# The order of ACT and DVE in the expert steps of a two-layer backbone, set to the program's own from the first 64-slot step on

## The chip, the cores and the metric

The kernel runs on one core of a Trainium2 chip. The time is device time in microseconds (us), from a run of the whole program; the median of three runs is compared. Engines: PE is TensorE's matmul side and PEld its weight loads, DVE is VectorE, ACT is ScalarE, POOL is GpSimd, SP is SyncE, which here only issues DMAs.

## What is computed

Two layers over 256 latent and 256 context tokens of width 1024, in float32. Each layer mixes tokens (Fourier, neighbourhood attention, short convolution, gated and projected) and then channels. The channel mixer of layer 0 is a dense SwiGLU; that of layer 1, which the change touches, is a top-2-of-8 mixture on the 256 latent tokens:

```python
def moe(h, w_router, w_gate, w_up, w_down):
    logits = (h @ w_router).astype(jnp.float32)
    top_val, top_idx = lax.top_k(logits, TOP_K)
    top_w = jax.nn.softmax(top_val, axis=-1)
    gates = jnp.sum(jax.nn.one_hot(top_idx, N_EXPERTS, dtype=jnp.float32) * top_w[..., None],
                    axis=-2).astype(h.dtype)
    out = jnp.zeros_like(h)
    for e in range(N_EXPERTS):
        out = out + gates[..., e:e + 1] * swiglu(h, w_gate[e], w_up[e], w_down[e])
    return out
```

## The kernel before

The layers ahead of the experts fill the first half of the time (to about 1000 us) and are not touched. Then come the experts. Each expert's tokens are gathered into slots by a matmul with a one-hot matrix, go through SwiGLU, and are scattered back and added. Experts 0, 2, 4, 6 ("A") have 128 slots, experts 1, 3, 5, 7 ("B") have 64. The width 3584 is cut into seven slices (`FE`), so a step is one expert and one slice `(e, f)`, and there are 56 steps. `expert_steps` puts four A steps first (`LEAD = 4`), then B and A steps in turn, 24 pairs, then the four B steps that are left.

**Weights.** A step needs six tiles of 1 MB: two each of the gate, up and down weights (`g`, `u`, `d`). They stream through a ring of 15 buffers named `raw` (`RING` = 12, and three of the pool `wraw`), loaded by SP in the order of use: load n+15 is issued when the buffer of load n is free. All 336 loads are one queue.

**A steps.** A `raw` tile of an A step is used in two units of 1024 columns. `Net.split` (L184, L187) writes for each unit a rounded copy `wh` (a cast on ACT) and the rest `wl = raw - wh` (a subtraction on DVE). PE then does three matmuls for each product in `mm3` (L191 with `wh`, L192 with `wl`, L193 with `wh`), six for a unit. There are four pairs of `wh`, `wl` buffers. `Stream.make` writes the split of a unit into the program at the place where `Stream.next` frees a buffer, that is where the unit four places ahead has just been used up. `raw` is free when the second unit's subtraction is done.

**B steps.** They use `raw` as it is, with no split: L1242 for gate and up, L1282 for down.

**One step** (`run`): `gate_up` computes gate and up; ACT applies Silu to the gate (L171) and DVE multiplies by the up product (L1248). In the middle of the *next* step's gate half, `turn` transposes the product on PE (L1254) and copies it out (for A: cast on ACT, L184, and subtraction on DVE, L187, both into tiles named `t`; for B: a copy on ACT, L1261). After that next step's gate and up, `down` multiplies it by the down weights and adds up in PSUM. So PE's row of work over one pair is: gate and up of B, down of A, gate and up of the next A, down of B. The twelve split units of a pair (four of A's down, eight of the next A's gate and up) stand in one stretch on PE, called the A run below; the rest of a pair uses B's tiles. At an expert's end there are also `scatter`, `add`, and before the next pair of experts `choose` and `gather`.

**What sets the order.** The framework has a scheduler that orders each engine's instructions by its own plan. Inside `manual_schedule(engines=...)` (written `order(...)` here) the engines named keep the order in which the program writes their instructions; the others are still ordered by the scheduler. Before, the loop over the 56 steps stood under `order(PE)` alone; the tail after it stands under PE and ACT (`TAIL`). Each engine runs its own queue in order, and an instruction that waits holds up what stands behind it on its engine.

`run` is called twice. The second call lies in a branch that is taken only when an expert has more tokens than slots; in the profiled execution no instruction of it ran.

Of the kernel before, what the change touches and what calls it, by code (L numbers as in the profile page):

```python
# [1037 lines left out]
def experts(net, pre, mo, res, mods, route, rt, ident, ones, tri, iot, sel8):  # L1038
# [27 lines left out]
    def choose(e, kind, more):  # L1066


        if e % 2 == 0:
            ofs[e // 2] = mo.tile([P, 2, 2, P], F32R, tag="of", name="of", bufs=2)  # L1070
        of = ofs[e // 2][:, :, e % 2]
        base = (P if RANKS[e] is None else CAPS[RANKS[e]]) if more else 0
        for t in range(2):
            p = column(2 + t, e)
            if base:
                pb = mo.tile([P, 1], F32, tag="pb", name="pb", bufs=4)
                nc.vector.tensor_scalar(pb, p, -float(base), None, op0=ALU.add)
                p = pb
            o, i = of[:, t], iot
            if kind == "B":  # L1080
                o, i = o.rearrange("p (a b) -> p a b", a=2), iot[:, None, :P // 2].to_broadcast([P, 2, P // 2])
            mask = sel[:, t, 0:1] if RANKS[e] is None else column(t, e)
            nc.vector.tensor_scalar(o, i, p, mask, op0=ALU.is_equal, op1=ALU.mult)
# [92 lines left out]
    def gather(kinds, *places):  # L1176

        wide = [P if kinds[e] == "A" else P // 2 for e in places]
        m, c0 = sum(wide), places[0] % 2 * P
        of, n = ofs[places[0] // 2], 512 // m  # L1180
        for e in places:
            if kinds[e] == "B":
                xb[e] = mo.tile([P, KD, P // 2], F32, tag="xb", name="xb", bufs=2)
        for k0 in range(0, KD, n):
            pm, ks = net.bank(), range(k0, k0 + n)
            for k in ks:
                for j, r in enumerate(rows):
                    for t in range(2):
                        nc.tensor.matmul(pm[:, (k - k0) * m:(k - k0 + 1) * m], r[:, t, k * P:(k + 1) * P],  # L1189
                                         of[:, t].rearrange("p a b -> p (a b)")[:, c0:c0 + m],  # L1190
                                         start=j == t == 0, stop=j == t == 1)
            todo = [(e, k, pm[:, (k - k0) * m + i * wide[0]:][:, :w], mods[:, 3 * KD + k, 0:1])
                    for k in ks for i, (e, w) in enumerate(zip(places, wide))]
            for e, k, src, sh in todo:
                nc.scalar.activation(xa[0][:, k] if kinds[e] == "A" else xb[e][:, k], src, AF.Identity, bias=sh)
            for e, k, src, sh in todo:
                if kinds[e] == "A":
                    nc.vector.scalar_tensor_tensor(xa[1][:, k], src, sh, xa[0][:, k].bitcast(F32),
                                                   op0=ALU.add, op1=ALU.subtract)

    def prepare_end(e):

        of = ofs[e // 2][:, :, e % 2].bitcast(F32)
        pm = net.bank()
        for t in range(2):
            nc.tensor.transpose(pm[:, t * P:(t + 1) * P], of[:, t], ident)
        for t in range(2):
            nc.tensor.matmul(pm[:, 2 * P:2 * P + 1], of[:, t], column(4 + t, e), start=t == 0, stop=t == 1)
        oht = mo.tile([P, S], F32R, tag="oht", name="oht", bufs=2)
        nc.vector.tensor_copy(oht, pm[:, :S])  # L1210
        gs = mo.tile([P, 1], F32, tag="gs", name="gs", bufs=2)
        nc.vector.tensor_copy(gs, pm[:, 2 * P:2 * P + 1])
        return oht, gs

    def run(st, kinds, more, Sums):
# [7 lines left out]
        def gate_up(e, f, between):  # L1223
            pg = [net.bank(), net.bank()]
            t = sg[e, f] = net.t2()
            whole = kinds[e] == "B"
            n = 256 if whole else 512
            for i, name in enumerate("gu"):
                for kk in range(4):
                    if not whole:  # L1230
                        h, lo = st.next(name, e, f)
                        for j in range(2):
                            k, c = 2 * kk + j, slice(j * 512, j * 512 + 512)
                            net.mm3(pg[i], xa[0][:, k], xa[1][:, k], h[:, c], lo[:, c], k == 0, k == KD - 1)
                    else:

                        if kk % 2 == 0:
                            w = st.next(name, e, f)
                        for k in (2 * kk, 2 * kk + 1):
                            for j in range(2):  # L1240
                                c = (k % 4) * 512 + j * 256
                                nc.tensor.matmul(pg[i][j * half:(j + 1) * half, :256], xb[e][:, k], w[:, c:c + 256],  # L1242
                                                 start=k == 0, stop=k == KD - 1)
                    if (i, kk) in between:
                        between[i, kk]()
                if i == 0:
                    net.act(t[:, :n], pg[0][:, :n], AF.Silu)
            nc.vector.tensor_mul(t[:, :n], t[:, :n], pg[1][:, :n])  # L1248

        def turn(e, f):  # L1250
            pt = net.bank()
            n = 4 if kinds[e] == "A" else 2
            for j in range(n):
                nc.tensor.transpose(pt[:, j * P:(j + 1) * P], sg[e, f][:, j * P:(j + 1) * P], ident)  # L1254
            if n == 4:
                ih, il = net.t2(F32R), net.t2(F32R)
                net.split(ih, il, pt)
                parts[e, f] = ih, il
            else:
                x = parts[e, f] = net.t2()  # L1260
                nc.scalar.copy(x[:, :n * P], pt[:, :n * P])  # L1261
# [41 lines left out]
        def add(e, n):  # L1303

            oht, _ = ends[e]
            for q in (2 * n, 2 * n + 1):
                pm = net.bank()
                for j in range(2):
                    c = slice((2 * q + j) * P, (2 * q + j + 1) * P)
                    o = pm[:, j * S:(j + 1) * S]  # L1310
                    nc.tensor.matmul(o, y[e][:, 0, c], oht, start=True, stop=False)  # L1311
                    nc.tensor.matmul(o, y[e][:, 1, c], oht, start=False, stop=True)  # L1312
                for j in range(2):
                    k = 2 * q + j
                    nc.vector.scalar_tensor_tensor(
                        res[:, k], pm[:, j * S:(j + 1) * S], mods[:, 5 * KD + k, 0:1], res[:, k],
                        op0=ALU.mult, op1=ALU.add)

        order = lambda *engines: net.tc.manual_schedule(engines=set(engines))
        y = {}  # L1320
        with order(PE):
            for i, (e, f) in enumerate(steps):
                between, after = {}, []
                if i:
                    between[0, 1] = lambda: turn(*steps[i - 1])
                if i > 1 and steps[i - 2][1] == FE - 1:
                    for n in range(2):
                        between[0, 2 + n] = lambda n=n: add(steps[i - 2][0], n)
                if f == 2:
                    between[1, 1] = lambda: ends.update({e: prepare_end(e)})  # L1330
                if i == 0 and not more:
                    between[1, 1] = rest
                if "B" in kinds:

                    if i == 1:
                        between[1, 1] = lambda: choose(1, kinds[1], more)
                    if i == 2:
                        after.append(lambda: gather(kinds, 1))
                    if e % 2 == 0 and e < NE - 2 and f == 4:
                        between[1, 1] = lambda: [choose(x, kinds[x], more) for x in (e + 2, e + 3)]  # L1340
                    if e % 2 == 0 and e < NE - 2 and f == FE - 1:
                        after.append(lambda: gather(kinds, e + 2, e + 3))
                elif e < NE - 1:
                    if f == 4:
                        between[1, 1] = lambda: choose(e + 1, kinds[e + 1], more)
                    if f == FE - 1:
                        after.append(lambda: gather(kinds, e + 1))
                gate_up(e, f, between)
                for x in after:
                    x()  # L1350
                last = {}
                if i == len(steps) - 1:
                    last[0, 1] = lambda: turn(e, f)
                if i:
                    down(*steps[i - 1], last)
        with order(*TAIL):
            sums = Sums()
            down(*steps[-1])
# [107 lines left out]
```

## Time and profile before

| | us |
|---|---|
| median of three runs | 1886.62 (1885.18 to 1889.72) |
| the profiled execution, its own time | 1888.95 |
| its span, first to last instruction | 1887.2 |
| PE busy | 1836.3 (97%) |
| PEld busy | 1438.6 (76%) |
| DVE busy | 1174.3 (62%) |
| ACT busy | 816.8 (43%) |
| DMA, whole span | 514.69 MB, mean 273 GB/s |

The chain of work that ended last lies on PE for 95% of the span, on DVE for 3% and on ACT for 1%. In the page's slices the DMA engines are busy at 9 tenths and 390 to 420 GB/s from slice 24 on, which is the stage of the experts; the granted TensorE clock is at 9 tenths or more in every slice but the last.

A row of a busy group gives busy time, the mean of one instruction in ns, and the idle time of the engine just before it with what ended it. Matmuls overlap: a 128x512 matmul takes 0.39 us by its row, and the next one starts 0.23 us after it.

### The profile page before, as it was taken

How to read it: one execution, taken by the hardware profiler on the slowest of the kernel's cores; microseconds unless marked ns; L12 is line 12 of the kernel's file. 1: busy time of each engine (PE TensorE's matmuls, PEld its weight loads, DVE VectorE, ACT ScalarE, POOL GpSimd, SP SyncE). 2: the span in 40 equal slices, each digit the busy share in tenths (PEclk: the TensorE clock that was granted, in tenths of full speed). 3: DMA queues.
4: the chain of work that ended last, by engine and by line, in shares of the span. 5: the costliest groups of instructions: out<-in, count | busy, mean ns of one | idle time of the engine just before them, and what ended most of it. 6: DMA issues, size and time to landing. Idle time of an engine off the chain costs nothing.

```text
span 1887.2 us, 26227 instructions
## 1 busy us (share of the span) xinstructions
PE 1836.3 (97%) x10254; PEld 1438.6 (76%) x10254; DVE 1174.3 (62%) x1723; ACT 816.8 (43%) x1181; POOL 23.4 (1%) x49
## 2 busy tenths in 40 slices
PE   7999999999999999999999999999999999999997
PEld 5787888888888888988998876766676666766664
DVE  4668577869677463668668855655565555646452
ACT  4546323343222223455446754544444444545431
POOL 0000000000000000001000000000000000000000
PEclk9999999999999999999999999999999999999998
DMA  9323345525547472345666899999999999999992
GB/s 363 112 90 103 121 159 176 194 96 201 175 159 266 156 253 88 127 135 193 234 246 240 340 409 419 420 421 419 416 388 417 415 397 396 414 419 418 401 414 99
DMA packets 74356, 514.69 MB, mean 273 GB/s; under 512 B 8433, under 2 KB 8561, under 8 KB 14449
## 3 DMA queue, kind: packets, MB, share of 16 engines
q1 hardware_dynamic: 69840, 491.84, 66.8%
q0 software_dynamic: 4240, 20.97, 3.3%
q8 instruction: 82, 1.34, 0.3%
q14 instruction: 50, 0.40, 0.1%
q10 hardware_dynamic: 144, 0.13, 0.0%
HBM read 509.76 MB, written 1.05 MB: 271 GB/s over the span
## 4 chain that ended last, share of the span: by engine, by line
PE 95%; DVE 3%; ACT 1%; issue 1%; DMA 0%; DVEq 0%; SPq 0%; ACTq 0%
PE ps L192 24%; PE ps L191 24%; PE ps L193 23%; PE ps L1242 11%; PE ps L1282 5%; DVE wl L187 1%; PE ps L1254 1%; PE ps L1189 1%; PE ps L656 1%; PE ps L645 1%; PE ps L621 1%; PE ps L1311 0%; DMA res<-in_xT 0%; PE ps L1312 0%; PE ps L343 0%
## 5 line engine op out<-in xcount | busy, mean ns | idle before, releaser
L184 ACT CAST wh<-raw 128x1024 fp32r<-128x1024 f32 (+1 forms) x524 | 536.9, 1048 | 568.0 <-PE ps L192 360.6
L187 DVE TENSOR_TENSOR wl<-raw,wh 128x1024 fp32r<-128x1024 f32 (+1 forms) x524 | 621.2, 1218 | 203.0 <-ACT wh L184 195.5
L191 PE MATMUL ps<-hh,wh 128*128 128x512 f32 (+1 forms) x1024 | 362.0, 355 | 1.7 <-ACT hh L171 1.7
L192 PE MATMUL ps<-hl,wh 128*128 128x512 f32 (+1 forms) x1024 | 362.4, 354 | 0.8 <-DVE hl L434 0.6
L193 PE MATMUL ps<-hh,wl 128*128 128x512 f32 (+1 forms) x1024 | 361.8, 354 | 0.0
L192 PEld LDWEIGHTS ps<-hl,wh 128*128 128x128 f32 x1024 | 195.0, 190 | 27.7 <-DVE hl L434 1.4
L191 PEld LDWEIGHTS ps<-hh,wh 128*128 128x128 f32 x1024 | 193.6, 190 | 28.9 <-ACT hh L171 2.1
L193 PEld LDWEIGHTS ps<-hh,wl 128*128 128x128 f32 x1024 | 194.8, 190 | 26.5
L1242 PE MATMUL ps<-raw,xb 128*64 128x256 f32 x1792 | 207.1, 381 | 0.0
L364 DVE CUSTOM_DVE_ANT_0 junk<-raw,csb,early 128x1024 bf16<-128x1024 f32 x128 | 164.3, 1283 | 35.2 <-DMA raw<-in_w_at 32.3
L1242 PEld LDWEIGHTS ps<-raw,xb 128*64 128x64 f32 x1792 | 125.0, 137 | 76.2 <-issue 20.3
L191 PE MATMUL ps<-wh,xh 128*128 128x512 f32 x448 | 177.4, 396 | 0.0
L192 PE MATMUL ps<-wl,xh 128*128 128x512 f32 x448 | 176.5, 394 | 0.0
L193 PE MATMUL ps<-wh,xl 128*128 128x512 f32 x448 | 175.0, 391 | 0.0
L1248 DVE TENSOR_TENSOR t<-t,ps 128x512 f32<-128x512 f32 (+1 forms) x56 | 31.0, 554 | 141.1 <-PE ps L1242 97.7
L192 PE MATMUL ps<-wl,t 128*128 128x512 f32 x224 | 89.4, 399 | 23.6 <-DVE wl L187 23.6
L1282 PE MATMUL ps<-raw,t 128*64 128x512 f32 x448 | 102.2, 598 | 0.0
L192 PEld LDWEIGHTS ps<-wl,xh 128*128 128x128 f32 x448 | 84.2, 188 | 22.6 <-DVE wl L187 5.2
L191 PEld LDWEIGHTS ps<-wh,xh 128*128 128x128 f32 x448 | 84.1, 188 | 16.6
L193 PEld LDWEIGHTS ps<-wh,xl 128*128 128x128 f32 x448 | 84.1, 188 | 16.6
L184 ACT CAST t<-ps 128x512 fp32r<-128x512 f32 x28 | 16.4, 585 | 178.3 <-PE ps L1254 178.3
L191 PE MATMUL ps<-wh,t 128*128 128x512 f32 x224 | 90.2, 403 | 0.0
(232 smaller groups left out, 2229.4 us busy)
## 6 DMA issues: line engine op xcount, KB each, us to landing
raw<-in_moe_d SPq DMA_DIRECT2D x110, 1024.0 KB, 9.0
raw<-in_moe_u SPq DMA_DIRECT2D x108, 1024.0 KB, 9.0
raw<-in_moe_g SPq DMA_DIRECT2D x106, 1024.0 KB, 8.7
raw<-in_w_at SPq DMA_DIRECT2D x40, 1024.0 KB, 5.1
raw<-in_w_gb SPq DMA_DIRECT2D x32, 1024.0 KB, 5.1
raw<-in_w_gu SPq DMA_DIRECT2D x22, 1024.0 KB, 5.0
raw<-in_w_in SPq DMA_DIRECT2D x20, 1024.0 KB, 5.2
a<-in_w_a SPq DMA_DIRECT2D x16, 512.0 KB, 11.1
```

What stands on the lines that cost most here:

```text
L184: c = self.nc.scalar.copy(h, src)
L187: self.nc.vector.tensor_sub(lo, src, h.bitcast(F32))
L191: nc.tensor.matmul(ps, wh, xh, start=start, stop=False)
L192: nc.tensor.matmul(ps, wh, xl, start=False, stop=False)
L193: nc.tensor.matmul(ps, wl, xh, start=False, stop=stop)
L364: nc.vector.tensor_tensor_reduce(junk, w[:, j * D:(j + 1) * D], csb[s], 1.0, bada[:, l, m + j:m + j + 1], ALU.mult, ALU.add, mods[l][:, m ...
L621: nc.tensor.matmul(banks[qt][:, :nk], qs[2 * c + j][:, i, s * S + qt * P:s * S + qt * P + P], ks[2 * c + j][:, k0:T], start=i == 0, stop=i ...
L645: nc.tensor.transpose(tr[:, i * P:(i + 1) * P], p[:, i * P:(i + 1) * P], ident)
L656: nc.tensor.matmul(po[64 * j:64 * j + 64, :S], v(k0 + i)[:, (2 * c + j) * 64:(2 * c + j) * 64 + 64], pts[c, s, j][:, i, :], start=i == 0, ...
L1242: nc.tensor.matmul(pg[i][j * half:(j + 1) * half, :256], xb[e][:, k], w[:, c:c + 256], start=k == 0, stop=k == KD - 1)
L1248: nc.vector.tensor_mul(t[:, :n], t[:, :n], pg[1][:, :n])
L1282: nc.tensor.matmul(py[e][n][j * half:(j + 1) * half], x[:, c:c + half], w[:, k * 512:(k + 1) * 512], start=f == 0 and i == 0, stop=f == FE ...
```

## The change

The body of the loop becomes a function `step(i, e, f)`, word for word the same. It is then called under two orders: steps 0 to 3 under `order(PE)`, as before, and steps 4 to 55, from the first 64-slot step on, under `order(PE, ACT, DVE)`. The tail is as it was.

```diff
-        with order(PE):
-            for i, (e, f) in enumerate(steps):
-                between, after = {}, []
-                if i:
-                    between[0, 1] = lambda: turn(*steps[i - 1])
...
-                gate_up(e, f, between)
...
-                if i:
-                    down(*steps[i - 1], last)
+        def step(i, e, f):
+            between, after = {}, []
+            if i:
+                between[0, 1] = lambda: turn(*steps[i - 1])
...
+            gate_up(e, f, between)
...
+            if i:
+                down(*steps[i - 1], last)
+
+
+        for engines, todo in (((PE,), range(LEAD)), ((PE, ACT, DVE), range(LEAD, len(steps)))):
+            with order(*engines):
+                for i in todo:
+                    step(i, *steps[i])
         with order(*TAIL):
```

The queues of PE, SP and POOL hold the same instructions in the same order as before. Those of ACT and DVE are reordered. The place shown is a plain pair of steps (slices of experts 3 and 4) with no expert's end in it. Of the tiles, `wh` and `wl` are the split weights; the `t` tiles of L171 and L1248 are Silu's output and the product, 256 wide for B and 512 wide for A; the `t` of L184 and L187 and of L1261 are the turned products of A and of B.

ACT before, from B's Silu to the next B's Silu:

```order
L171 ACTIVATE t_11843<-ps 128x256
L184 CAST wh<-raw 128x1024 x8
L1261 COPY t_11957<-ps 128x256
L184 CAST wh<-raw 128x1024 x2
L171 ACTIVATE t_11931<-ps 128x512
L184 CAST wh<-raw 128x1024 x2
L184 CAST t_12067<-ps 128x512
L171 ACTIVATE t_12053<-ps 128x256
```

ACT after, the same stretch:

```order
L171 ACTIVATE t_11846<-ps 128x256
L184 CAST wh<-raw 128x1024 x5
L1261 COPY t_11960<-ps 128x256
L184 CAST wh<-raw 128x1024 x2
L171 ACTIVATE t_11934<-ps 128x512
L184 CAST wh<-raw 128x1024 x5
L184 CAST t_12070<-ps 128x512
L171 ACTIVATE t_12056<-ps 128x256
```

Of a pair's twelve casts two stood between A's Silu and the cast of the turned A, and now five do: the casts of the next `down` of A (the first units of the next A run) have moved from behind B's Silu to ahead of the turn.

DVE before, the same stretch, from B's product to two products later:

```order
L1248 TENSOR_TENSOR t_11843<-t_11843,ps 128x256
L187 TENSOR_TENSOR wl<-raw,wh 128x1024 x12
L1248 TENSOR_TENSOR t_11931<-t_11931,ps 128x512
L187 TENSOR_TENSOR t_12068<-ps,t_12067 128x512
L1248 TENSOR_TENSOR t_12053<-t_12053,ps 128x256
```

DVE after:

```order
L1248 TENSOR_TENSOR t_11846<-t_11846,ps 128x256
L187 TENSOR_TENSOR wl<-raw,wh 128x1024 x11
L1248 TENSOR_TENSOR t_11934<-t_11934,ps 128x512
L187 TENSOR_TENSOR wl<-raw,wh 128x1024
L187 TENSOR_TENSOR t_12071<-ps,t_12070 128x512
L1248 TENSOR_TENSOR t_12056<-t_12056,ps 128x256
```

Before, all twelve subtractions of an A run stood between B's product and A's product. Now the row of subtractions is shifted by four units: the last three of the eleven and the one behind A's product belong to the next A run.

## Rows read from the trace of the kernel before

**Rows 1.** Waits of PE, 1050 to 1890 us: total us, times, longest.

```profile
PE ps L192 <- DVE wl L187: 23.6, 18, 1.4
```

**Rows 2.** Timeline of PE at a plain pair's turn: start, us, instruction, idle before.

```profile
1317.08 0.39 PE L192 MATMUL ps<-wl,xh 128*128 128x512 f32 x1
1317.31 0.39 PE L193 MATMUL ps<-wh,xl 128*128 128x512 f32 x1
1317.63 3.65 PE L1282 MATMUL ps<-raw,t 128*64 128x512 f32 x16
...
1323.53 5.40 PE L1242 MATMUL ps<-raw,xb 128*64 128x256 f32 x48
1328.86 0.49 PE L191 MATMUL ps<-wh,t 128*128 128x512 f32 x1
1330.65 0.50 PE L192 MATMUL ps<-wl,t 128*128 128x512 f32 x1 [1.30 <-DVE wl L187]
```

**Rows 3.** Timeline of DVE over the same stretch.

```profile
1324.25 0.69 DVE L187 TENSOR_TENSOR t<-ps,t 128x512 fp32r<-128x512 f32 x1 [5.83 <-ACT t L184]
1329.04 0.42 DVE L1248 TENSOR_TENSOR t<-t,ps 128x256 f32<-128x256 f32 x1 [4.10 <-PE ps L1242]
1329.38 4.63 DVE L187 TENSOR_TENSOR wl<-raw,wh 128x1024 fp32r<-128x1024 f32 x4
```

**Rows 4.** Timeline of ACT over the same stretch.

```profile
1323.63 0.59 ACT L184 CAST t<-ps 128x512 fp32r<-128x512 f32 x1 [9.08 <-PE ps L1254]
1325.52 0.39 ACT L171 ACTIVATE t<-ps 128x256 f32<-128x256 f32 x1 [1.30 <-PE ps L1242]
1325.80 3.87 ACT L184 CAST wh<-raw 128x1024 fp32r<-128x1024 f32 x4
```

**Rows 5.** Timeline of PE: B's down starts, one plain pair later, and in an early pair.

```profile
1347.48 1.08 PE L1282 MATMUL ps<-raw,t 128*64 128x512 f32 x4
...
1106.31 0.65 PE L1282 MATMUL ps<-raw,t 128*64 128x512 f32 x2
...
1134.34 1.08 PE L1282 MATMUL ps<-raw,t 128*64 128x512 f32 x4
```

**Rows 6.** Timelines of DVE and ACT in the early pair.

```profile
1107.88 1.22 DVE L187 TENSOR_TENSOR wl<-raw,wh 128x1024 fp32r<-128x1024 f32 x1
1112.93 0.69 DVE L187 TENSOR_TENSOR t<-ps,t 128x512 fp32r<-128x512 f32 x1 [3.83 <-ACT t L184]
1117.72 0.42 DVE L1248 TENSOR_TENSOR t<-t,ps 128x256 f32<-128x256 f32 x1 [4.10 <-PE ps L1242]
...
1119.23 1.05 ACT L184 CAST wh<-raw 128x1024 fp32r<-128x1024 f32 x1 [4.64 <-PE ps L193]
1120.60 1.06 ACT L184 CAST wh<-raw 128x1024 fp32r<-128x1024 f32 x1 [0.31 <-PE ps L193]
```

**Rows 7.** Waits of PEld and of ACT, 1050 to 1890 us: total us, times, longest.

```profile
PEld ps L192 <- DVE wl L187: 34.3, 33, 1.7
...
ACT wh L184 <- DMA raw<-in_moe_d: 0.3, 1, 0.3
```

**Rows 8.** Stretches: us, busy time of PE, PEld, DVE, ACT, POOL, clock, DMA share, GB/s.

```profile
1100.00:1240.00 140.00, 138.70 (x809) 97.20 (x808) 80.03 (x93) 68.28 (x92) 0.00 (x0) 1.00 1.01 420
1097.00:1850.00 753.00, 729.44 (x4177) 505.14 (x4177) 418.18 (x474) 347.68 (x446) 0.00 (x0) 1.00 1.00 411
```

**Rows 9.** Single loads, issue and time to landing: at 1097.6, 1147.1, 1294.4, 1841.9.

```profile
DMA to landing us min/median/max: 9.8/9.8/9.8
...
DMA to landing us min/median/max: 13.9/13.9/13.9
...
DMA to landing us min/median/max: 8.8/8.8/8.8
...
DMA to landing us min/median/max: 8.2/8.2/8.2
```

**Rows 10.** PE's last down product (the last load is used by its last eight).

```profile
1863.84 5.37 PE L1282 MATMUL ps<-raw,t 128*64 128x512 f32 x24
```

More of the change, by code (lines that the diff above doesn't have):

```diff
@@ L1320, in run @@
         y = {}
-        with order(PE):
-            for i, (e, f) in enumerate(steps):
-                between, after = {}, []
-                if i:
-                    between[0, 1] = lambda: turn(*steps[i - 1])
[L1326 to L1347, printed above, removed]
-                gate_up(e, f, between)
[L1349 to L1353, printed above, removed]
-                if i:
-                    down(*steps[i - 1], last)
@@ new lines, in step @@
+        def step(i, e, f):
+            between, after = {}, []
+            if i:
+                between[0, 1] = lambda: turn(*steps[i - 1])
+            if i > 1 and steps[i - 2][1] == FE - 1:
+                for n in range(2):
+                    between[0, 2 + n] = lambda n=n: add(steps[i - 2][0], n)
+            if f == 2:
+                between[1, 1] = lambda: ends.update({e: prepare_end(e)})
+            if i == 0 and not more:
+                between[1, 1] = rest
+            if "B" in kinds:
+                if i == 1:
+                    between[1, 1] = lambda: choose(1, kinds[1], more)
+                if i == 2:
+                    after.append(lambda: gather(kinds, 1))
+                if e % 2 == 0 and e < NE - 2 and f == 4:
+                    between[1, 1] = lambda: [choose(x, kinds[x], more) for x in (e + 2, e + 3)]
+                if e % 2 == 0 and e < NE - 2 and f == FE - 1:
+                    after.append(lambda: gather(kinds, e + 2, e + 3))
+            elif e < NE - 1:
+                if f == 4:
+                    between[1, 1] = lambda: choose(e + 1, kinds[e + 1], more)
+                if f == FE - 1:
+                    after.append(lambda: gather(kinds, e + 1))
+            gate_up(e, f, between)
+            for x in after:
+                x()
+            last = {}
+            if i == len(steps) - 1:
+                last[0, 1] = lambda: turn(e, f)
+            if i:
+                down(*steps[i - 1], last)
```

## The prediction, made before the changed kernel had run

> **What bounds the kernel now.** I read the page first: PE is busy for 97% of the span and carries 95% of the chain that ended last, so time can only be won where PE stands still. Then the waits of PE, restricted to the stage of the experts [rows 1]: nearly all of them are one wait, L192 for a subtraction `wl` on DVE, 18 times, 23.6 us. The reader is to see that it is the first product of an A run that needs `wl`, once in most of the 24 pairs.
>
> Then the three timelines at one such place. PE ends B's gate and up and starts the A run at 1328.86 with `wh`, but its first product with `wl` comes at 1330.65 [rows 2]. DVE has been idle: it did the turned A from 1324.25 to 1324.94, then waited 4.10 us for PE to end B's up half, did B's product at 1329.04, and only then the first subtraction, at 1329.38 [rows 3]. ACT had waited 9.08 us for the turn, then for B's gate, and cast the first weights of the A run from 1325.80 on [rows 4]. Nothing forced these two so late: the four buffers were free once the A run before had ended, at about 1317.6, where B's down starts [rows 2]. The splits stood behind instructions that wait for B. So PE's wait is made by the order of two queues, not by their load (DVE is busy for 62%, ACT for 43%).
>
> Last, the DMA side. Loads of the experts land at 420 GB/s where the engines are kept full, and at 411 over the whole stage [rows 8]. ACT waited for a load once, for 0.3 us [rows 7]. The loads are thus early, but not by much bandwidth: this is what stands next in line.
>
> **What the change does, part by part.**
> *Order of the splits.* It adds and removes no instruction. PE, SP and POOL keep their queues. The four splits at the head of an A run go from behind B's Silu and product to ahead of the turned A. That very order is in the trace of before, in the first pairs: there the subtraction stands at 1107.88, ahead of the turned A at 1112.93; after B's product at 1117.72 DVE has nothing to catch up with, and ACT's next cast at 1119.23 waits for PE, not PE for it [rows 6]. From 1100 to 1240 us, some four pairs, PE stands still for 1.30 us in all, one wait [rows 8].
>
> The price of one wait can be taken in three ways. By idle time it is 1.30 us [rows 2], 23.6 us in all [rows 1]; this is the low bound. By starts it is 1.79 us from L191 to L192 where the next start normally follows after 0.23 (1317.08 to 1317.31) [rows 2], so 1.56. By whole pairs, from B's down to B's down, it is 1347.48 - 1317.63 = 29.85 us with the wait and 1134.34 - 1106.31 = 28.03 us in the early pair [rows 2, 5]: 1.82 us, which also takes in the restart behind the wait and a few short hesitations. PEld's own waits for `wl` sum to 34.3 us in 33 pieces [rows 7], the high bound. I take the pairs, since they are whole periods of the same work: 18 x 1.82 = 32.8 us.
>
> The matmuls' busy time would give the low bound. The Trainium skill (Trainium Kernel Development and Optimization, Performance Expectations) calls matmul busy time a bad metric, because matmuls are pipelined; by that, idle counted between busy rows is too small, and the sum goes by 32.8 rather than 23.6. The trace agrees: a row takes 0.39 us and the next starts after 0.23 [rows 2].
>
> *Instructions that now wait ahead of others.* On ACT the four early casts need their loads 8 us sooner (about 1317.6 instead of 1325.80). The load concerned was issued at 1294.4 and took 8.8 us [rows 9], so it is there at 1303.2, 14.4 us ahead. If a cast did wait, the turned A and B's Silu would be behind it, and PE wants these only at 1328.86 [rows 2], 11 us later. On DVE the product of A gets up to two subtractions ahead of it, each 1.22 us by the page; it is wanted by the turn, several us on. I cost both at nothing; the cover is the B step. Steps 0 to 3 and the tail keep their rules: nothing.
>
> *`raw` buffers.* Those of A's down are free some 9 us sooner, but SP issues in ring order and first needs those of B's gate and up, which PE frees at 1328.86 as before. Then the two loads go out at once instead of 3 to 5 us later. This fills small holes of the DMA, and costs nothing.
>
> **What is late next.** A pair needs 12 loads of 1.0486 MB, 12.58 MB: at 420 GB/s 29.96 us, and PE would want it in 28.03. So each plain pair eats 1.9 us of the loads' lead. The early pairs show it: time to landing went from 9.8 us (issue at 1097.6) to 13.9 (at 1147.1) [rows 9] while PE lost nothing. The pairs at an expert's end are longer on PE and give lead back. Over the stage: 753 us at 411 GB/s are 309.5 MB [rows 8]; at 420 they need 736.9 us, 16.1 less. The last load, issued at 1841.9 with 8.2 us [rows 9], lands at 1850.1 and can land at 1834.0 at best. Its use starts two thirds into the last 24 products, at 1867.4 [rows 10], and 19.8 us follow to the span's end. So the span cannot end before 1834.0 + 19.8 = 1853.8 by DMA, and not before 1887.2 - 32.8 = 1854.4 by PE. The two nearly meet: the 17.3 us by which the last load is early now would be used up but for 0.6. Since both bounds hold at every moment and not only at the end, I add 2.6 us: a span of 1857.0, a gain of 30.2.
>
> The Trainium skill (HBM Reference, Specifications (TRN2)) gives a core about 358 GB/s where both cores of a pair stream, and about 425 for one that streams alone, bounded by its 16 DMA engines. By 358 the 309.5 MB would need 865 us, more than now; the trace rules that out with 411 over 753 us. By 425 they need 728 us, and the DMA bound would be 1845 instead of 1853.8, an estimate. It speaks against a larger gain: the stage has little bandwidth left.
>
> **Rivals.**
> *DMA bounds it, and the lead cannot be used.* If loads are needed about as early as now (the casts that ACT does sooner, bursts of issues at the turn), only the DMA's holes are won: 16.1 us, 1887.2 - 16.1 = 1871.1, a median of 1870.5. For it: 411 against 420 GB/s. Against it: early pairs ran at 28.03 us with landing at 10 to 14 us.
> *A new wait in place of the old.* If the turned A came late enough for A's down, the gain would be eaten. DVE ended it at 1324.94, 3.9 us ahead of 1328.86 [rows 2, 3]; it would have to be 5.7 us later in every pair. Against it stands the early pair, where the cast of the turn starts when PE has transposed. Time: about 1886.6.
> *Slower: strict order breaks the stream of splits inside an A run.* A buffer freed by PE must be cast and subtracted within three units. Casts follow PE at 1.37 us a unit (1119.23 to 1120.60) [rows 6], so 4.1 us are there, and cast and subtraction take 0.3 + 1.06 + 1.22 = 2.6. ACT's Silu of A and copy of B now stand at fixed places among the casts, where the scheduler could move them. If the chain came to 4.1 + x, PE would lose x on each of 8 units in 24 pairs, 192x. It eats the gain from x = 0.17 us on; at x = 0.25 the sum is 48 - 32.8 = 15.2 us slower, 1901.8. Against it: the spare is 1.5 us, and Silu and copy together take about 1.
> *The order does not change what waits.* The queues as built show that it does, so it has no chance of its own.
>
> **How the numbers follow.** The profiled execution took 1888.95 us for a span of 1887.2, so 1.75 lie around it, and it is 2.33 us above the median of 1886.62. A gain of 30.2 makes 1858.75 of that execution and 1856.4 of the median. Chances: forecast (1850 to 1863) 0.61; DMA bound (1863 to 1878) 0.24; another wait in its place 0.08; slower 0.07. The low end is the bound 34.3 of the sum with a little for noise, 1850; the high end takes in the DMA rival with 3.5 us for what its rate may differ, 1874. A measurement of this kernel can tell about 0.3% (5.7 us) from no change. Faster by more than that: the first two cases, 0.85; within it 0.08; slower 0.07.
>
> **What would show it.** Right: the 18 waits of L192 for `wl` are gone; a plain pair takes 28 to 29 us from B's down to B's down; on DVE a subtraction stands between A's product and the turned A; DMA runs at about 420 GB/s from 1100 us to its last load, and time to landing rises above 14 us. DMA rival: waits of ACT's casts or of PE's L1242 for loads, and plain pairs near 30 us. Slower: L191 or L192 waits inside the A runs, eight in a pair. Wrong altogether: plain pairs stay at 29.85 us with the wait under another name.

## The result, and the profile after

| | before | after |
|---|---|---|
| median of the runs | 1888.17 us (1885.18 to 1889.73) | 1857.47 us (1856.34 to 1858.93) |
| ratio, 95% interval | | 0.984 (0.9823 to 0.9857) |
| profiled execution, span | 1887.2 us | 1854.6 us |
| B's first down to B's last (24 pairs) | 1106.31 to 1839.93: 733.62 us | 1103.10 to 1807.79: 704.69 us |

By the medians the kernel is faster by 30.7 us. Of the 32.6 us between the two spans 28.9 lie in the 24 pairs, 0.5 behind them, and 3.2 ahead of the first pair. These 3.2 are not the change's. They arise between 775 and 790 us, ahead of everything that it reorders: in both kernels PE waits there for 1.7 us (L191 for ACT, L171), and behind this wait the granted clock was 0.76 (775 to 782 us) and 0.78 (782 to 790) in the profiled execution of before, and 1.00 in that of after. That part differs from run to run: in the experiments that leave it as it is the first pair began between 1103.2 and 1109.6 us. I therefore read every kernel below by its pairs too.

The page of after, busy times and the chain that ended last:

```profile
PE 1824.3 (98%) x10254; PEld 1436.9 (77%) x10254; DVE 1180.6 (64%) x1723; ACT 827.3 (45%) x1181; POOL 23.4 (1%) x49
...
PE 92%; DMA 5%; DVE 2%; ACT 1%; issue 0%; SPq 0%; DVEq 0%; ACTq 0%
```

DMA, which held 0% of this chain before, now holds 5%. The waits of PE from 1050 to 1890 us, then the one of ACT that matters (total us, times, longest):

```profile
PE ps L1254 <- DVE t L1248: 1.5, 2, 0.9
PE ps L1189 <- DVE t L1248: 1.3, 1, 1.3
...
ACT wh L184 <- DMA raw<-in_moe_d: 22.0, 15, 4.7
```

The 18 waits of [rows 1] are gone. What stands in their place is small: three waits for A's product, L1248. ACT now waits for loads for 22.0 us where it waited for 0.3 [rows 7].

One plain pair on PE: B's down, the turn into the A run, the next B's down.

```profile
1399.40 3.65 PE L1282 MATMUL ps<-raw,t 128*64 128x512 f32 x16
...
1410.63 0.50 PE L191 MATMUL ps<-wh,t 128*128 128x512 f32 x1
1410.96 0.39 PE L192 MATMUL ps<-wl,t 128*128 128x512 f32 x1
...
1427.43 1.08 PE L1282 MATMUL ps<-raw,t 128*64 128x512 f32 x4
```

L192 follows L191 after 0.33 us where it took 1.79 [rows 2], and the pair takes 28.03 us, as the early pair did in the kernel before [rows 5]. DVE over the same turn:

```profile
1400.70 0.68 DVE L1248 TENSOR_TENSOR t<-t,ps 128x512 f32<-128x512 f32 x1
1401.30 1.22 DVE L187 TENSOR_TENSOR wl<-raw,wh 128x1024 fp32r<-128x1024 f32 x1
1406.02 0.69 DVE L187 TENSOR_TENSOR t<-ps,t 128x512 fp32r<-128x512 f32 x1 [3.50 <-ACT t L184]
1410.81 0.42 DVE L1248 TENSOR_TENSOR t<-t,ps 128x256 f32<-128x256 f32 x1 [4.10 <-PE ps L1242]
1413.40 2.59 DVE L187 TENSOR_TENSOR wl<-raw,wh 128x1024 fp32r<-128x1024 f32 x2 [2.17 <-ACT wh L184]
```

The fourth head subtraction is done at 1402.5, 8 us ahead of PE's L191. Behind B's product DVE has nothing to catch up with: it waits for ACT, and ACT for PE. Before, four head subtractions stood there [rows 3].

The DMA side, in the columns of [rows 8]:

```profile
1240.00:1818.00 578.00, 575.17 (x3334) 403.21 (x3334) 338.10 (x379) 282.46 (x348) 0.00 (x0) 1.00 1.01 421
```

421 GB/s, without a hole. The last load of all, whose time to landing was 8.2 us [rows 9], is issued at 1813.7 and takes

```profile
DMA to landing us min/median/max: 19.8/19.8/19.8
```

It lands at 1833.5 and is used at 1835.2: its lead, the time from landing to first use, fell from 17.2 to 1.7 us.

### The profile page after: what moved, and what is told of

Its sections match the earlier page's. It is cut to its first block, busy times and chain, and to the rows that moved or that the text cites. A ratio compares the mean times of both kernels' runs of the same rounds, so it can differ in the third digit from the quotient of the medians.

```text
span 1854.6 us, 26258 instructions
## 1 busy us (share of the span) xinstructions
PE 1824.3 (98%) x10254; PEld 1436.9 (77%) x10254; DVE 1180.6 (64%) x1723; ACT 827.3 (45%) x1181; POOL 23.4 (1%) x49
## 4 chain that ended last, share of the span: by engine, by line
PE 92%; DMA 5%; DVE 2%; ACT 1%; issue 0%; SPq 0%; DVEq 0%; ACTq 0%
PE ps L191 23%; PE ps L192 23%; PE ps L193 23%; PE ps L1242 10%; PE ps L1282 5%; DMA raw<-in_moe_d 2%; PE ps L1254 1%; DMA raw<-in_moe_u 1%; DMA raw<-in_moe_g 1%; PE ps L656 1%; PE ps L645 1%; PE ps L621 1%; PE ps L1189 1%; PE ps L1311 0%; DMA res<-in_xT 0%; PE ps L1312 0%
## 5 line engine op out<-in xcount | busy, mean ns | idle before, releaser
L184 ACT CAST wh<-raw 128x1024 fp32r<-128x1024 f32 (+1 forms) x524 | 545.2, 1049 | 654.1 <-PE ps L192 360.2
L187 DVE TENSOR_TENSOR wl<-raw,wh 128x1024 fp32r<-128x1024 f32 (+1 forms) x524 | 630.9, 1218 | 250.0 <-ACT wh L184 216.9
L191 PE MATMUL ps<-hh,wh 128*128 128x512 f32 (+1 forms) x1024 | 361.2, 355 | 1.7 <-ACT hh L171 1.7
L192 PE MATMUL ps<-hl,wh 128*128 128x512 f32 (+1 forms) x1024 | 360.9, 353 | 0.7 <-DVE hl L434 0.6
L193 PE MATMUL ps<-hh,wl 128*128 128x512 f32 (+1 forms) x1024 | 360.4, 353 | 0.0
L191 PEld LDWEIGHTS ps<-hh,wh 128*128 128x128 f32 x1024 | 192.7, 189 | 29.2 <-ACT hh L171 2.1
L192 PEld LDWEIGHTS ps<-hl,wh 128*128 128x128 f32 x1024 | 193.6, 189 | 27.4 <-DVE hl L434 1.4
L193 PEld LDWEIGHTS ps<-hh,wl 128*128 128x128 f32 x1024 | 193.4, 189 | 26.5
L191 PE MATMUL ps<-wh,xh 128*128 128x512 f32 x448 | 177.3, 396 | 0.0
L193 PE MATMUL ps<-wh,xl 128*128 128x512 f32 x448 | 174.7, 390 | 0.0
L192 PE MATMUL ps<-wl,xh 128*128 128x512 f32 x448 | 174.7, 390 | 0.0
L1248 DVE TENSOR_TENSOR t<-t,ps 128x512 f32<-128x512 f32 (+1 forms) x56 | 30.8, 550 | 111.3 <-PE ps L1242 111.3
L193 PEld LDWEIGHTS ps<-wh,xl 128*128 128x128 f32 x448 | 84.1, 188 | 17.8
L192 PEld LDWEIGHTS ps<-wl,xh 128*128 128x128 f32 x448 | 84.2, 188 | 16.3
L191 PEld LDWEIGHTS ps<-wh,xh 128*128 128x128 f32 x448 | 84.1, 188 | 16.3
L191 PE MATMUL ps<-wh,t 128*128 128x512 f32 x224 | 90.3, 403 | 0.0
L193 PE MATMUL ps<-wh,t 128*128 128x512 f32 x224 | 87.4, 390 | 0.0
L192 PE MATMUL ps<-wl,t 128*128 128x512 f32 x224 | 87.4, 390 | 0.0
```

The source lines that it names most:

```text
L184: c = self.nc.scalar.copy(h, src)
L187: self.nc.vector.tensor_sub(lo, src, h.bitcast(F32))
L191: nc.tensor.matmul(ps, wh, xh, start=start, stop=False)
L192: nc.tensor.matmul(ps, wh, xl, start=False, stop=False)
L193: nc.tensor.matmul(ps, wl, xh, start=False, stop=stop)
```

## Experiments

Theory: PE's waits were made by the place of the four head splits (the first four splits of an A run) in the queues of ACT and DVE, at 1.82 us a pair, and the loads' spare pays for the shorter pairs nearly to the last microsecond. Rivals: one engine's order is what counts, or strict order as such; late loads had made the waits; the gain is bounded by the loads' rate.

| kernel | median, us | ratio to before, 95% | 24 pairs, us |
|---|---|---|---|
| before | 1887.35 | | 733.62 |
| after, second series | 1858.77 | 0.985 (0.9835 to 0.9865) | 705.14 |
| e1, PE and DVE ordered | 1899.89 | 1.0068 (1.0046 to 1.0089) | 744.70 |
| e2, PE and ACT ordered | 1870.88 | 0.9909 (0.9893 to 0.9926) | 717.03 |
| e3, half of the steps | 1870.08 | 0.9911 (0.9894 to 0.9927) | 717.36 |
| e4, from step 0 on | 1865.01 | 0.9878 (0.9862 to 0.9895) | 706.16 |
| e5, after, smaller loads | 1854.31 | 0.9825 (0.9806 to 0.9844) | 701.47 |
| e6, before, smaller loads | 1862.98 | 0.9872 (0.9854 to 0.9891) | 709.26 |
| e7, after, extra loads | 1882.14 | 0.9977 (0.9967 to 0.9987) | 729.30 |
| e8, before, extra loads | 1887.09 | 1.0002 (0.9993 to 1.0012) | 733.63 |
| e9, splits behind B's product | 1892.75 | 1.0028 (1.0018 to 1.0039) | 739.32 |
| e10, splits behind B's Silu | 1856.65 | 0.9843 (0.983 to 0.9857) | 701.47 |
| e11, splits behind A's product | 1855.84 | 0.9838 (0.9825 to 0.9852) | 701.44 |

Each ratio is to the runs of the kernel before in its own series; the first row is the last series. The last column is the time from the first to the last of B's downs, as in the table above.

### The place of the four splits, and nothing else (e9, e10, e11)

These three keep the changed kernel and move only the place at which the program writes the four head splits. PE, SP and POOL have the same rows in the same order as in after. The common part of the edit, and the line that differs (e9; in e11 it reads `if not whole:`, in e10 the same two lines stand behind B's Silu):

```diff
+        if self.on and self.made < len(self.units):
+            self.load(self.units[self.made][0] + self.ahead)
...
+            if "B" in kinds and i > LEAD and kinds[e] == "A" and i + 1 < len(steps):
+                st.on = True
+                st.upto(next(n for n, (x, _) in enumerate(st.units) if st.plan[x][0] == ("d", e, f)))
...
             nc.vector.tensor_mul(t[:, :n], t[:, :n], pg[1][:, :n])
+            if whole:
+                st.upto()
```

Expected of e9:

> The changed kernel, all three engines in the program's order, with one thing put back: in the pairs from step 6 on the program writes the four head splits of an A run behind B's product. The queues of PE, SP and POOL stay word for word; on DVE all twelve subtractions of a run stand between B's product and A's, as in the kernel before. Theory (the place of these four is the whole cause): PE waits at L192 for wl once in about 22 pairs, a plain pair takes 29.85 us again, the late loads get their lead back. 22 to 23 waits at 1.8 us are 40 to 41, less the 3.4 us of the waits for A's product: 1857.5 + 37, 1888 to 1898. Rival (the gain came from the strict order as such, from something else that it tidied): the time stays near 1857 to 1865.

Waits of PE in e9 (its lines stand lower by 2 to 4: L194 is after's L192, L189 is L187):

```profile
PE ps L194 <- DVE wl L189: 31.2, 24, 1.3
```

Its turn on PE, and DVE there:

```profile
1432.87 0.49 PE L193 MATMUL ps<-wh,t 128*128 128x512 f32 x1
1434.67 0.50 PE L194 MATMUL ps<-wl,t 128*128 128x512 f32 x1 [1.30 <-DVE wl L189]
...
1433.06 0.42 DVE L1250 TENSOR_TENSOR t<-t,ps 128x256 f32<-128x256 f32 x1 [4.10 <-PE ps L1244]
1433.39 3.49 DVE L189 TENSOR_TENSOR wl<-raw,wh 128x1024 fp32r<-128x1024 f32 x3
```

This is the picture of [rows 2, 3] again, 24 times, and it eats more than the whole gain: 1892.75 us, as the theory had it. Strict order as such gains nothing; the place of four splits does. The price is purer here than in the kernel before: 739.32 - 701.44 = 37.9 us for 24 waits, 1.58 each.

Expected of e10 and e11:

> The same with the four head splits written between B's Silu and B's product: on DVE four subtractions stand behind the turned A and ahead of B's product, eight behind it; A's product stands ahead of all. PE, SP and POOL as in the changed kernel. Theory: the casts follow B's Silu at about 1.05 us each, the first subtraction ends some 2.5 us behind the Silu, just ahead of PE's first L192 (which comes about 3.0 us behind the Silu), so no wait for wl or one below 0.4 us; the loads are wanted some 8 us later than in the changed kernel, and neither A's product nor the turn stands behind a late load, so the 3.4 us of waits go: 1853.5 to 1857. Rival (B's product, now behind four subtractions, frees its banks too late for the next matmuls): waits of PE for B's product in each pair, 1865 to 1885.

> The same with the four head splits written behind A's product and still ahead of the turned A, on DVE in one row of four. The casts on ACT stay where the changed kernel has them. Theory (the 3.4 us of PE's waits come from A's product standing behind subtractions whose weights land late): these waits go, and the turned A, which still stands behind the late casts and subtractions, is needed only when PE has done B's gate and up, so it has some 5 us to spare: 1853.5 to 1857. Rival (the late loads only move PE's wait on to the turned A, L191 or L193): 1856 to 1862.

In both, all waits of PE for a subtraction or for A's product are gone (two waits for loads, some 1 us in all, are left behind the pairs), and the pairs take 701.5 us. Both medians lie in the range of their theory. DVE in e10, four subtractions between the turned A and B's product:

```profile
1406.08 0.69 DVE L189 TENSOR_TENSOR t<-ps,t 128x512 fp32r<-128x512 f32 x1 [5.83 <-ACT t L186]
1408.70 4.63 DVE L189 TENSOR_TENSOR wl<-raw,wh 128x1024 fp32r<-128x1024 f32 x4 [1.93 <-ACT wh L186]
1413.25 0.41 DVE L1252 TENSOR_TENSOR t<-t,ps 128x256 f32<-128x256 f32 x1
```

So it is enough that the subtractions are ahead of B's product; they need not be ahead of the turned A. B's product is 2.4 us later than in after, and nobody waits for it. The casts come later too, and wait for loads for only 0.6 us in all. In e11 A's product stands ahead of the four; ACT and DVE late in the run, at a load that lands late:

```profile
1721.23 1.99 ACT L186 CAST wh<-raw 128x1024 fp32r<-128x1024 f32 x2 [4.26 <-DMA raw<-in_moe_d]
...
1720.88 0.69 DVE L1250 TENSOR_TENSOR t<-t,ps 128x512 f32<-128x512 f32 x1 [2.65 <-PE ps L195]
1722.31 4.84 DVE L189 TENSOR_TENSOR wl<-raw,wh 128x1024 fp32r<-128x1024 f32 x4 [0.74 <-ACT wh L186]
1727.39 0.69 DVE L189 TENSOR_TENSOR t<-ps,t 128x512 fp32r<-128x512 f32 x1 [0.25 <-ACT t L186]
```

ACT waits for loads even longer than in after (29.9 us in 14 waits for down weights), but only the turned A is late, and PE wants it last. Both kernels are shorter than after by 3.2 us in the pairs. Their intervals overlap with after's, so the times alone do not set them apart; the pairs do, since these repeat to within 0.5 us between two profiles of after (704.69 and 705.14).

### One engine ordered and the other not (e1, e2)

```diff
-        for engines, todo in (((PE,), range(LEAD)), ((PE, ACT, DVE), range(LEAD, len(steps)))):
+        for engines, todo in (((PE,), range(LEAD)), ((PE, DVE), range(LEAD, len(steps)))):
```

> Only PE and DVE follow the program's order from step 4 on; ACT is left to the scheduler. As built, DVE's queue is then that of the changed kernel word for word, and ACT's differs by one cast in a pair: six casts instead of five stand between B's Silu and its copy, one instead of two behind it. Theory (PE's waits come from the place of the head splits in the two queues, and one engine's order pulls the other's along, since a subtraction that stands early needs its cast early): the 18 waits of PE's L192 for wl are gone, plain pairs take 28.0 us, the time is that of the changed kernel, 1856 to 1860. Rival (ACT's own order is needed): waits of PE for wl or for the turn come back, pairs of 29 to 30 us, 1872 to 1888.

Neither came: 1899.89, slower than before. The plain pairs are at 28.03 us, as the theory has it. The loss is at the expert ends. Waits of PE:

```profile
PE ps L1189 <- DVE t L1248: 18.0, 3, 6.3
PE ps L1254 <- DVE t L1248: 12.4, 3, 4.1
```

One of the six, on ACT, DVE and PE:

```profile
1285.89 1.04 ACT L184 CAST wh<-raw 128x1024 fp32r<-128x1024 f32 x1
1292.71 0.69 ACT L1298 ACTIVATE y<-ps,gs 128x512 fp32r<-128x512 f32 x1 [5.78 <-PE ps L1282]
1294.43 0.69 ACT L1298 ACTIVATE y<-ps,gs 128x512 fp32r<-128x512 f32 x1 [1.03 <-PE ps L1282]
...
1296.08 3.50 DVE L187 TENSOR_TENSOR wl<-raw,wh 128x1024 fp32r<-128x1024 f32 x3 [7.89 <-ACT wh L184]
1299.49 0.68 DVE L1248 TENSOR_TENSOR t<-t,ps 128x512 f32<-128x512 f32 x1
...
1300.23 0.66 PE L1254 MATMUL ps<-early,t 128*128 128x128 f32 x4 [4.12 <-DVE t L1248]
```

ACT's own order put the head casts behind L1298, which waits for B's last down on PE. DVE's fixed order has three head subtractions ahead of A's product. So A's product waits for casts that wait for PE, and PE waits for A's product. I had looked only at ACT's queue in a plain pair when I wrote what to expect. The two orders must agree; in after they do, since both are the program's.

e2 is the same line with `(PE, ACT)`.

> Only PE and ACT follow the program's order from step 4 on; DVE is left to the scheduler. As built, ACT's queue is that of the changed kernel word for word. On DVE all four head subtractions stand ahead of the turned A, as in the changed kernel, but A's product stands ahead of them and not behind three of them. Theory: the 18 waits are gone, plain pairs take 28.0 us; and since A's product no longer stands behind a subtraction whose weights land late, the three waits of PE for that product in the changed kernel (0.6 to 1.5 us by starts, 3.4 us in all) go too, unless the cast of the turned A, which stays behind the same late casts on ACT, takes their place: 1854 to 1857. Rival (DVE's own order is what removes the waits): pairs of 29 to 30 us and 1872 to 1888. Rival (the loads' rate is the bound at the end): no better than the changed kernel, 1857 to 1859.

1870.88: the theory failed, and the time lies just below the 1872 of the first rival, though not for its reason. 21 of the 24 pairs are as short as in e11, and three, each with a wait of L193 for the turned A (9.9 us in all), lose 15.6 us together. DVE's own order and PE at one of them:

```profile
1343.37 0.69 DVE L1248 TENSOR_TENSOR t<-t,ps 128x512 f32<-128x512 f32 x1 [2.65 <-PE ps L193]
1353.58 0.42 DVE L1210 CAST oht<-ps 128x256 fp32r<-128x256 f32 x1 [9.53 <-PE ps L1208]
...
1355.01 4.62 DVE L187 TENSOR_TENSOR wl<-raw,wh 128x1024 fp32r<-128x1024 f32 x4
1359.55 0.68 DVE L187 TENSOR_TENSOR t<-ps,t 128x512 fp32r<-128x512 f32 x1
...
1360.28 0.80 PE L193 MATMUL ps<-wh,t 128*128 128x512 f32 x1 [3.50 <-DVE t L187]
```

In all three the scheduler put L1210, which waits for a product in the middle of B's up, ahead of the head splits and of the turned A. Again one queue's head waits for PE with PE's own next input behind it.

### Half of the steps, and all of them (e3, e4)

```diff
+        for engines, todo in (((PE,), range(LEAD)), ((PE, ACT, DVE), range(LEAD, 30)), ((PE,), range(30, len(steps)))):
```

> All three engines follow the program's order for steps 4 to 29, and PE alone for steps 30 to 55. Theory (each wait has its own price and the gain adds up): the pairs up to about 1470 us have no wait for wl and give 12.5 us, which is what these pairs are shorter by in the changed kernel's trace; the later ones keep it. 1888.2 less 12.5 and about 1 us ahead of the pairs: 1873 to 1876, with 9 to 11 waits of L192 for wl left, all behind 1470 us. Rival (the gain is bounded by the loads' rate over the whole stage, so that half of the waits would be enough to use most of it up): 1858 to 1868. Rival (what is won early is lost again in longer waits later): 1880 to 1888, with waits above 1.4 us.

1870.08, better than I said, because I had counted the pairs wrongly: the ordered steps reach two pairs further, to B's down at 1516 us. Waits left:

```profile
PE ps L192 <- DVE wl L187: 11.7, 9, 1.3
```

Nine of 18 waits are gone and the pairs are 16.3 us shorter, 1.81 a wait. Later pairs are back at 29.83 us. The gain adds up wait by wait and is not given back.

```diff
+        for engines, todo in (((PE, ACT, DVE), range(len(steps))),):
```

> All three engines follow the program's order in all 56 steps, the first four (A alone) included. In the first four steps DVE's small table instructions and the weights' subtractions change places: the table work for the next experts stands in one row ahead of some subtractions. Theory: from step 4 on nothing changes, so the time is that of the changed kernel plus what PE loses in steps 0 to 3, where some fifteen small instructions of DVE stand ahead of subtractions that PE waits for: 0 to 6 us, 1857 to 1864. Rival (the first steps had waits by the scheduler's order as well): 1850 to 1856, better than the changed kernel.

1865.01, a little past the theory's upper end. The pairs take 706.16 us, but the first one begins at 1112.9, 9.8 us later than in after. Some 3 of these are the fallen clock at 778 us, which this execution shares with that of before; the rest goes with one wait of PE. That wait, and the stretch, in the columns of [rows 8]:

```profile
PE ps L192 <- DVE wl L187: 3.4, 1, 3.4
...
1020.00:1060.00 40.00, 36.10 (x156) 29.34 (x155) 34.88 (x56) 30.41 (x33) 0.00 (x0) 0.91 0.79 280
```

In after PE is busy for all of these 40 us, at a clock of 1.00. So in the first steps the program's order is the worse one.

### What the loads cost now (e5 to e8)

Smaller loads (e5 from after, e6 from before; B's gate and up leave half of their weights out):

```diff
-            src = lambda x=x, e=e, f=f, hf=hf: a[f"moe_{x}"][expert(e), f, hf]
-            plan.append(((x, e, f), src, 2 if kinds[e] == "A" else 1, 2048, pools[n % len(pools)]))
+            m = 1024 if x != "d" and kinds[e] == "B" else 2048
+            src = lambda x=x, e=e, f=f, hf=hf, m=m: a[f"moe_{x}"][expert(e), f, hf, :, :m]
+            plan.append(((x, e, f), src, 2 if kinds[e] == "A" else 1, m, pools[n % len(pools)]))
...
-                                c = (k % 4) * 512 + j * 256
+                                c = (k % 2) * 512 + j * 256
```

> The changed kernel with half-size loads for the gate and up weights of B: 1024 of 2048 columns, 4 loads of 0.52 MB in each of 28 steps, 58.7 MB less of 309.5 MB; each half is multiplied twice, so B's gate and up use part of the weights twice and the rest not at all. Instructions of PE, ACT and DVE are as many and as large as before. Theory (PE is the bound, the loads cost only the small waits at the late casts): ACT's waits for loads (22.0 us) and the waits of PE for A's product (3.4 us by starts) go, pairs stay at 28.0 us: 1853 to 1856. Rival (loads bound the stage, as 420 GB/s without a pause suggests): 58.7 MB at 420 GB/s are 140 us of transfers, so PE would be the bound again, but well below: 1835 to 1850.

1854.31, as the theory had it, with the queues of PE, ACT and DVE row by row those of after. ACT's waits for loads and PE's for A's product are gone, and the pairs take 701.47 us, to 0.03 us those of e11, which has all its loads. So 58.7 MB less is worth 3.2 us: the loads cost after no more than those three waits.

> The kernel before with the same half-size loads for the gate and up weights of B, 58.7 MB less, each half multiplied twice. Theory (the 18 waits are made by the order of the queues): they stay, each as long as now, pairs stay at 29.85 us: 1885 to 1890. Rival (the early splits stood late because their loads were late): waits shrink and the time falls towards 1857 to 1875.

1862.98, and the theory as I had put it failed. The time lies in the rival's range, but the rival is not what it shows: the scheduler reckons with the size of a load when it sets the order of ACT and DVE, and with smaller loads it built other queues. In ten pairs of the middle (those that end with B's down at 1253 to 1518 us) DVE now has, of its own accord, the four head subtractions ahead of the turned A, as in after, and each of these pairs takes what it takes in after. In four late pairs it left all four behind B's product, and PE waits, though ACT waits for no load in the whole stage:

```profile
PE ps L192 <- DVE wl L187: 5.2, 4, 1.3
```

So e6 moved two things at once, loads and order, and by itself tells only that order and waits go together. e7 and e8 have the queues of PE, ACT and DVE of after and before row by row, and only more transfers:

```diff
+        if not more:
+            extra = mo.tile([P, 256], F32, name="extra")
+            for j in range(80):
+                nc.gpsimd.dma_start(extra, st.extra[j % FE, 0, :, :256])
```

> The kernel before with the same 80 extra loads, 10.5 MB. Theory: at 411 GB/s with 17.2 us of lead at the last load, the DMA side has 16 to 17 us to spare in the stage, so 25 us of extra transfers cost at most 8 us, and use the spare up: 1888 to 1897. The difference to the run of the changed kernel with the same loads is what the shorter pairs took from the loads' spare. Rival (the engines take other queues' loads for nothing): 1886 to 1889. Rival (each extra load delays a load that PE waits for): 1905 to 1913.

> The changed kernel with 80 extra loads of 0.131 MB (10.5 MB in all), issued from POOL's queue one behind the other into a buffer that nobody reads, from the first expert step on. At 420 GB/s they take 25 us of the DMA engines' time. Theory (DMA has no time left in the stage: the last load had 1.7 us of lead): most of it shows, 15 to 25 us, 1872 to 1883, with waits of ACT's casts for loads several times as long as 22.0 us. Rival (the rate of the expert loads is set by their own queue and not by the engines, so another queue's loads fit beside them): 1857 to 1861.

e8 took 1887.09, no slower than before (1887.33 in this series), with the same waits and pairs (733.63 against 733.62 us):

```profile
PE ps L192 <- DVE wl L187: 23.6, 18, 1.4
```

The theory's 1888 to 1897 failed. The time is the rival's, but the loads were not taken for nothing. 25 us of transfers fitted in: part of them went ahead of the pairs (from 1000 to 1100 us DMA moved 319 GB/s, against 292 before), part came out of the last load's lead, 5.7 us where it was 17.2, and part filled holes. The kernel before had that much room, and its waits have nothing to do with how early loads land. In e7 the same transfers cost after 1882.14 - 1857.47 = 24.7 us by the medians of two series, and 24.6 by the pairs, in the range of the theory. Its waits:

```profile
PE ps L1260 <- DVE t L1254: 9.9, 4, 4.4
PE ps L1191 <- DVE t L1254: 7.4, 2, 4.2
...
ACT wh L184 <- DMA raw<-in_moe_d: 58.6, 27, 7.8
```

(Its lines stand lower: L1260, L1191 and L1254 are after's L1254, L1189 and L1248.) These six waits of PE sum to 17.3 us. More is lost because the granted clock fell behind them (0.50 from 1387 to 1392 us, say; see the last section), so that the loss comes so near the 25 us of transfers is partly chance. But next to nothing of the loads' spare is left in after.

## Why the prediction was right, step by step

**The waits and their cause.** Right, and shown: e9 puts the four splits back and has the waits back; e8 and e3 leave no room for late loads or for a gain that is given back.

**18 x 1.82 = 32.8 us.** With no other wait in the way (e11) the pairs are 733.62 - 701.44 = 32.2 us shorter. The term was right to 0.6 us. What I put into one price has two parts, though. The wait at the turn costs 1.58 (e9). My 1.56 by starts came near it because two errors cancel: at the turn L192 follows L191 after 0.33 us without a wait and not after 0.23, and the start behind the wait comes after 0.34 us (e9, 1434.67 to 1435.01) where after has 0.23. These 0.11 us are the restart. The other 0.24 of the 1.82 are the short hesitations that I had named. In the kernel before PEld's 33 waits [rows 7] are 18 of 1.6 to 1.7 us at the turn and 15 of 0.34 to 0.36, nearly all late in an A run; ACT and PEld there, in the pair of [rows 2]:

```profile
1339.16 0.37 ACT L1261 COPY t<-ps 128x256 f32<-128x256 f32 x1 [1.89 <-PE ps L1254]
1339.43 2.00 ACT L184 CAST wh<-raw 128x1024 fp32r<-128x1024 f32 x2
...
1344.76 0.19 PEld L192 LDWEIGHTS ps<-wl,xh 128*128 128x128 f32 x1 [0.34 <-DVE wl L187]
```

A cast stood behind the copy of the turned B, which waits for PE, and the row of splits came out some 0.2 us late: the pair of before from 1196.7 us on, which has such a hesitation and no wait at the turn, takes 28.27 us and in after 28.03. In e9, where one more cast stands ahead of that copy, PEld waits for a subtraction 24 times, 1.61 us each, and not once more. The change mended both, and the whole pair had both in it.

**The low bound by idle time, 23.6 us.** Rightly not taken: in the 24 pairs PE's busy time fell as well, from 710.06 to 701.86 us, with the same 4059 instructions. So part of what a wait costs stands in the rows as work. (The page's totals differ by 12.0 us, but 3.6 of these lie ahead of the first pair, where the clock was another.) The Trainium skill (Trainium Kernel Development and Optimization, Performance Expectations) calls the busy time of matmuls a bad metric for how close a kernel is to roofline, because matmuls are pipelined; the trace agrees, with these 8.2 us.

**Early casts "at nothing".** This is the step that failed, by 3.2 us. I had read the load's 14.4 us of lead from the kernel before, and named ACT's turned A and Silu as what stands behind a late cast. But the same text says that each plain pair eats 1.9 us of that lead. By 1570 us it was gone. And what is wanted first behind a late cast is on DVE, where I had put at most two subtractions ahead of A's product and three stand there. ACT, DVE and PE at the longest of the three waits in after:

```profile
1570.37 2.00 ACT L184 CAST wh<-raw 128x1024 fp32r<-128x1024 f32 x2 [2.40 <-DMA raw<-in_moe_d]
...
1571.45 3.71 DVE L187 TENSOR_TENSOR wl<-raw,wh 128x1024 fp32r<-128x1024 f32 x3 [2.23 <-ACT wh L184]
1575.08 0.68 DVE L1248 TENSOR_TENSOR t<-t,ps 128x512 f32<-128x512 f32 x1
...
1575.81 0.47 PE L1189 MATMUL ps<-of,rh 128*128 128x192 f32 x2 [1.32 <-DVE t L1248]
```

Three subtractions at a late load, A's product behind them, PE behind that: e11 takes A's product out from behind them and wins the 3.2 us back.

**The loads as the next bound.** Right. I had the last load land at 1834.0 at best, with 0.6 us to spare; it landed at 1833.5 with 1.7, in an execution whose first pair began 3.2 us earlier than that of before. The 2.6 us that I added since both bounds hold at every moment stand for the 3.2 that were lost, without naming how; that they are near each other is luck. In e11 the last load is used at the moment it lands, and the span is 1852.1 us: there the loads end the stage. The rival by which their lead could not be used fell: it was used, all but 1.7 us. Of the Trainium skill's two rates (HBM Reference, Specifications (TRN2)), about 425 GB/s for a core that streams alone and about 358 for two, the first is the nearer: 421 over 578 us.

**The other rivals.** A wait in place of the old did come, at a tenth of its size. The stream of splits inside an A run did not break: no wait of L191 or L192 is left in the stage.

**The sum.** 30.2 us forecast, 30.7 measured by the medians. The second series gives 28.6, so an agreement to 0.5 us is closer than these runs can tell. In the profiled pair of executions the parts are 32.2 less 3.2 in the pairs, 0.5 behind them, and the 3.2 ahead of them that the change did not make.

## What to carry to other kernels

Where an engine that is far from full makes the busiest one wait, look at what its queue holds ahead of the late instruction: if that waits for the busiest engine, the order is the fault, and a whole period with and without the wait gives its price better than the idle time. When orders are fixed by hand, fix those of all engines that hand work to each other, by the same rule, and put what the busiest engine wants first ahead of what may be late (here A's product ahead of splits whose loads have no lead left). And compare the built queues, row by row, before reading an experiment: a smaller load alone made the scheduler write another order.

## What the runs showed that I had not expected

A long wait of PE can cost much more than itself. In e2, in the columns of [rows 8], the stretches around the wait of 3.50 us:

```profile
1356.00:1360.30 4.30, 0.52 (x2) 0.20 (x2) 4.30 (x6) 0.00 (x0) 0.00 (x0) 0.84 1.02 423
1360.30:1362.00 1.70, 1.70 (x4) 1.41 (x5) 0.26 (x1) 0.00 (x0) 0.00 (x0) 0.50 0.99 410
...
1366.00:1368.00 2.00, 2.00 (x11) 1.60 (x10) 1.36 (x2) 1.05 (x2) 0.00 (x0) 1.00 1.01 422
```

After it the granted clock is 0.50, the lower level of 1.2 GHz, and back at 1.00 from 1366 us. The pair lost 7.0 us, 39.48 instead of 32.44. e4 shows 0.50 behind its wait of 3.4 us (1032.5 to 1036), e1 a fallen clock behind each of its waits (4 us and more) and e7 behind its waits of 2.5 us and more, while the waits of 1.3 us of the kernel before left it at 1.00. The length of the wait alone does not tell, though. Of two more waits of 3.18 us in e2 one left the clock at 1.00 (1572.2 to 1578 us) and cost its pair 3.5 us; behind the other it was 0.50 (1782.5 to 1785.5), and the pair lost 5.1. And behind the 1.7 us at 778 us, which all kernels share, it fell in the profiled executions of before and e4 and stayed at 1.00 in those of after, e8, e10 and e11; a second execution of after had it fall too. What decides it no run here shows. With the clock in it, e1's six waits of 30.4 us in all made the pairs 43.3 us longer than those of e11, and a rival with fewer but longer waits could have been dearer than I priced it.
